# A macaron decoder layer on one core: first rows in turns, norms by Ln and Exp, later a22 splits

## Chip, cores and metric

One core of a Trainium2 chip runs one launch of the kernel. The metric is the device time of that launch in microseconds (us); less is better.

## The reference, cut to what matters

```python
def layer_norm(x, g, b):
    mu = mean(x); var = mean(square(x - mu))
    return (x - mu) * rsqrt(var + 1e-5) * g + b
def swiglu(x, wg, wu, wd):
    return (silu(x @ wg) * (x @ wu)) @ wd
x = layer_norm(ALPHA * x + 0.5 * swiglu(x, ffn1...), ln1)   # D_MODEL 1024, D_FF 2816
proj = x @ w_in                                             # RWKV-7 heads | gated short conv
...
x = layer_norm(ALPHA * x + mix @ w_out, ln2)
x = layer_norm(ALPHA * x + 0.5 * swiglu(x, ffn2...), ln3)   # 512 prompt + 32 sample columns, float32
```

## The kernel before

Activations lie with features on the partitions: z is [128, 8, 544], eight feature tiles by T=544 columns, worked in two halves, HALF = (0, 256) and (256, 544). A float32 product is built from three matmuls in fp32r: weights and inputs are split into a high and a low part, and wh by xh, wh by xl, wl by xh are added in PSUM (mm3, L149 to L151; prod, L464 to L466). The high part is an ACT copy, the low part a DVE subtraction: wsplit (L133, L134) for weights, split (L137, L138) for the rest. So each weight block passes SP's DMA queue, a raw tile, ACT, DVE and then PE.

A feed-forward has 22 tiles of 128 hidden rows in chunks of 4, 4, 4, 4 and 6. The first chunk's up rows are plain products (up, L312 to L338: gate, Silu on ACT, up, a product on DVE), row by row: first() runs the first half's columns, main() the rest. All other work goes in 2x2 blocks with seven products for eight (as Strassen does); each product is 12 matmuls of 272 columns for an "up" item (pairs and its tail, L469 to L545) and 6 for a "down" item (downs, L548 to L581). An item u0 to u5 needs four split weights: b (the block a22), a, y and x. They come from two raw tiles: x and a are loaded by SP (load, L407 and L409), b is split from x (into a tile hlb of its own, L137 and L138), then a DMA on POOL's queue adds the block a11 to x in place (L437), then the y part needs two DVE adds on x (L430, L431). Item results pass through cpb copies on ACT (L525, L531, L534).

What sets the order is a planner: plan() lays the products out in time and gives each part of an item a due time, so many products ahead of its use; feed(), called ahead of each product, issues the loads of the next items as long as fewer than n raw tiles are held, and put() for each part that is due. The engines take their instructions in the order in which they were issued.

```python
LEAD = dict(b=18, a=9, x=7, y=5)
LEAD_B = {0: 25, 1: 23}
```

layer_norm (L191 to L225) takes one half: the column sums by matmuls with ones (L196, L197), the subtraction (L203), squares on ACT (L204), the variance by matmuls (L208, when pair is off), Sqrt on ACT (L218), RECIPROCAL on DVE (L219), a scaling per tile on DVE (L223); the sink then adds the bias and splits into xhl (to_x, L230 on ACT, L231 on DVE) or adds it and stores (to_y, L238). ACT has one function table loaded at a time; L122 and L194 load the next one ahead. Norms are woven with other work (weave): matmuls are issued between their steps; only the last norm, half 0 of ln3 (256 columns), has nothing beside it. rb and xb2 hold multiples of the biases, since z itself is kept without them.

The start (L629 to L646) loads the gate weight of row 0 in four pieces, in turns with x, then the up weight of row 0, both weights of row 1 and the second half of x.

Of the kernel before, what the change touches and what calls it, by code (L numbers as in the profile page):

```python
# [12 lines left out]
F32 = mybir.dt.float32  # L13
# [48 lines left out]
def body(ctx: ExitStack, tc: tile.TileContext, xT, gu1, wd1, win, wo_c, wo_0, wo_1, gu2, wd2, lora, w0, vec, cst,  # L62
# [23 lines left out]
    def col(v, i):  # L86
        return vc[:, v + i:v + i + 1]
# [103 lines left out]
    def layer_norm(z, h, gcol, bcol, epsv, q, rs, s1, sink, pair=True):  # L191
        c0, c1 = HALF[h]
        n = c1 - c0
        ACT.activation(warm, s1[:, 0:1], AF.Sqrt, scale=0.0, bias=one)  # L194
        m = sm()
        PE.matmul(m[:, :n], ones, s1[:, :n], start=True, stop=False)  # L196
        PE.matmul(m[:, :n], ones, z[:, KD - 1, c0:c1], start=False, stop=True)  # L197
        yield 800
        v = sm() if not pair else None
        for j in range(4):  # L200
# [17 lines left out]
        ACT.activation(rs[:, :n], v[:, :n], AF.Sqrt, bias=epsv)  # L218
        DVE.reciprocal(rs[:, :n], rs[:, :n])  # L219
        yield 2600  # L220
        for d in range(KD):
            zz = z[:, d, c0:c1]
            DVE.scalar_tensor_tensor(zz, zz, col(gcol, d), rs[:, :n], op0=OP.mult, op1=OP.mult)  # L223
            sink(d, zz, col(bcol, d), c0, c1)
            yield 800  # L225

    def to_x(z, spill):
        def sink(d, zz, b, c0, c1):
            hi, lo = xhl[:, 0, d, c0:c1], xhl[:, 1, d, c0:c1]
# [1192 lines left out]
```

## Time and profile before

| | us |
|---|---|
| median of 3 runs | 1134.11 (1131.58 to 1135.72) |
| the profiled execution | 1136.22 |
| its span | 1134.5 |

The span is the profiled part of the execution. PE runs matmuls, PEld loads their weights, DVE, ACT and POOL are the other engines, SP only issues DMAs (SPq is its queue). The mean granted clock of PE over the span is 0.995 of full speed. An idle time is put down to the instruction or DMA that ended it ("<-").

### The profile page before, as it was taken

How to read it: one execution, taken by the hardware profiler on the slowest of the kernel's cores; microseconds unless marked ns; L12 is line 12 of the kernel's file. 1: busy time of each engine (PE TensorE's matmuls, PEld its weight loads, DVE VectorE, ACT ScalarE, POOL GpSimd, SP SyncE). 2: the span in 40 equal slices, each digit the busy share in tenths (PEclk: the TensorE clock that was granted, in tenths of full speed). 3: DMA queues.
4: the chain of work that ended last, by engine and by line, in shares of the span. 5: the costliest groups of instructions: out<-in, count | busy, mean ns of one | idle time of the engine just before them, and what ended most of it. 6: DMA issues, size and time to landing. Idle time of an engine off the chain costs nothing.

```text
span 1134.5 us, 22909 instructions
## 1 busy us (share of the span) xinstructions
PE 1099.5 (97%) x9300; PEld 1045.3 (92%) x9300; DVE 851.6 (75%) x1586; ACT 586.2 (52%) x1066; POOL 172.6 (15%) x282
## 2 busy tenths in 40 slices
PE   8999999999999999999999999999999999999995
PEld 7999999999999999898789878899999999999994
DVE  6677888878776857754677467988889887877755
ACT  6545555555553576653345344657455555545513
POOL 0122131302100022230011100001312212130000
PEclk9999999999999999999999999999999999999998
DMA  8558495867753242261228422443866859587302
GB/s 274 129 99 183 110 215 143 170 153 160 175 144 105 81 139 72 52 122 58 68 71 222 119 79 93 169 149 75 166 154 145 192 131 207 130 170 164 98 1 79
DMA packets 97625, 149.31 MB, mean 132 GB/s; under 512 B 35056, under 2 KB 58992, under 8 KB 97520
## 3 DMA queue, kind: packets, MB, share of 16 engines
q1 hardware_dynamic: 70320, 111.67, 32.7%
q0 software_dynamic: 27200, 36.18, 20.4%
q8 instruction: 73, 1.20, 0.4%
q14 instruction: 32, 0.26, 0.1%
HBM read 129.17 MB, written 9.75 MB: 122 GB/s over the span
## 4 chain that ended last, share of the span: by engine, by line
PE 64%; DVE 11%; DMA 10%; issue 9%; ACT 5%; POOL 0%; SPq 0%; ACTq 0%; POOLq 0%; DVEq 0%
PE mm L149 7%; PE mm L464 7%; PE mm L466 6%; PE mm L465 6%; PE mm L151 6%; PE mm L150 6%; DMA raw<-in_gu 5%; PE sm L464 4%; PE sm L466 4%; PE sm L465 4%; DVE hl L134 3%; ACT hl L133 2%; PE sm L929 1%; DMA raw<-in_wd 1%; PE sm L208 1%
## 5 line engine op out<-in xcount | busy, mean ns | idle before, releaser
L134 DVE TENSOR_TENSOR hl<-raw,hl 128x1024 fp32r<-128x1024 f32 (+3 forms) x228 | 269.6, 1189 | 65.6 <-ACT hl L133 64.7
L133 ACT ACTIVATE hl<-raw 128x1024 fp32r<-128x1024 f32 (+3 forms) x228 | 231.5, 1027 | 79.6 <-DVE raw L431 33.3
L149 PE MATMUL mm<-xhl,hl 128*128 128x256 f32 (+1 forms) x768 | 236.2, 308 | 6.8 <-ACT xhl L137 5.0
L151 PE MATMUL mm<-xhl,hl 128*128 128x256 f32 (+1 forms) x768 | 225.6, 295 | 1.4 <-DVE hl L134 1.4
L150 PE MATMUL mm<-xhl,hl 128*128 128x256 f32 (+1 forms) x768 | 224.4, 292 | 0.6 <-DVE xhl L231 0.3
L149 PEld LDWEIGHTS mm<-xhl,hl 128*128 128x128 f32 x768 | 146.0, 190 | 16.1 <-ACT xhl L137 5.3
L151 PEld LDWEIGHTS mm<-xhl,hl 128*128 128x128 f32 x768 | 145.7, 190 | 5.2 <-DVE hl L134 2.2
L150 PEld LDWEIGHTS mm<-xhl,hl 128*128 128x128 f32 x768 | 146.4, 191 | 4.0 <-DVE xhl L138 0.9
L464 PE MATMUL sm<-xhl,hl 128*128 128x272 f32 x432 | 124.8, 289 | 0.0
L466 PE MATMUL sm<-xhl,hl 128*128 128x272 f32 x432 | 124.7, 289 | 0.0
L465 PE MATMUL sm<-xhl,hl 128*128 128x272 f32 x432 | 124.7, 289 | 0.0
L464 PE MATMUL mm<-tv,hl 128*128 128x272 f32 x288 | 84.5, 293 | 4.6 <-ACT cpb L525 3.5
L466 PE MATMUL mm<-tv,hl 128*128 128x272 f32 x288 | 84.2, 292 | 0.0
L465 PE MATMUL mm<-tv,hl 128*128 128x272 f32 x288 | 83.1, 288 | 0.0
L466 PEld LDWEIGHTS sm<-xhl,hl 128*128 128x128 f32 x432 | 81.7, 189 | 0.0
L464 PEld LDWEIGHTS sm<-xhl,hl 128*128 128x128 f32 x432 | 81.5, 189 | 0.0
L465 PEld LDWEIGHTS sm<-xhl,hl 128*128 128x128 f32 x432 | 81.5, 189 | 0.0
L443 POOL DMA_DIRECT2D raw<-in_wd x32 | 39.3, 1495 | 271.4 <-DVE hlb L138 269.6
L437 POOL DMA_DIRECT2D raw<-in_gu x36 | 43.4, 1206 | 239.5 <-DVE hlb L138 132.9
L464 PEld LDWEIGHTS mm<-tv,hl 128*128 128x128 f32 x288 | 54.7, 190 | 6.3 <-ACT cpb L525 4.4
L464 PE MATMUL mm<-hhl,hl 128*128 128x272 f32 x192 | 57.0, 302 | 1.9 <-ACT sv L570 1.8
L464 PE MATMUL sm<-hhl,hl 128*128 128x272 f32 x192 | 55.8, 291 | 0.0
(367 smaller groups left out, 2811.8 us busy)
## 6 DMA issues: line engine op xcount, KB each, us to landing
raw<-in_gu SPq DMA_DIRECT2D x86, 512.0 KB, 5.1
raw<-in_gu POOLq DMA_DIRECT2D x36, 512.0 KB, 7.4
raw<-in_wd SPq DMA_DIRECT2D x32, 512.0 KB, 4.8
raw<-in_win SPq DMA_DIRECT2D x26, 512.0 KB, 3.8
raw<-in_wd POOLq DMA_DIRECT2D x32, 256.0 KB, 6.8
raw<-in_wd SPq DMA_DIRECT2D x16, 384.0 KB, 3.4
z<-cpb POOLq DMA_DIRECT2D x16, 272.0 KB, 9.0
z<-sv POOLq DMA_DIRECT2D x16, 272.0 KB, 5.9
```

Of the source, the lines that this page charges most:

```text
L133: ACT.activation(hl[:, 0, a:b], raw[:, a:b], AF.Copy)
L134: DVE.tensor_tensor(hl[:, 1, a:b], raw[:, a:b], hl[:, 0, a:b].bitcast(F32), op=OP.subtract)
L149: PE.matmul(out, wh, src[:, 0, k, c0:c1], start=(start and i == 0), stop=False)
L150: PE.matmul(out, wh, src[:, 1, k, c0:c1], start=False, stop=False)
L151: PE.matmul(out, wl, src[:, 0, k, c0:c1], start=False, stop=(stop and i == n - 1))
L208: PE.matmul(v[:, :n], ones, qq[:, i, :], start=(j == 0 and i == 0), stop=(j == 3 and i == 1))
L437: POOL.dma_start(x.rearrange("p (s c) -> p s c", s=2), bass.AP(tensor=a11.tensor, offset=a11.offset, ap=[[2 * D, P], [P * 2 * D, 2], [1, 5 ...
L443: POOL.dma_start(four(x)[:, i], bass.AP(tensor=a11.tensor, offset=a11.offset, ap=[[DFF, P], [P * DFF, 2], [1, 256]]), accum_op=OP.add)
L464: PE.matmul(out, wh, src(0, i), start=(first and i == 0), stop=False, skip_group_check=True)
L465: PE.matmul(out, wh, src(1, i), start=False, stop=False, skip_group_check=True)
L466: PE.matmul(out, wl, src(0, i), start=False, stop=(i == n - 1), skip_group_check=True)
L929: PE.matmul(q[r0:r0 + m, o:o + nn], lhs, rhs, start=True, stop=True)
```

## The change

- First rows: rows 0 and 1 of the first feed-forward are computed in turns. The four weights arrive in pieces of two, two and four k tiles, and first_rows runs, for each pair of k tiles, six matmuls for each of four PSUM accumulators. Four matmuls on a zeroed tile and the load of the Silu table stand ahead. The up and gate weights of rows 2 and 3 are loaded ahead of the first down items, and feed() may hold five raw tiles early, not two.
- The a22 split: the lead of part b is 15 products, not 18, for the fourth and later items of a chunk.
- Norms: 1/sqrt is Exp of -0.5 times Ln, both on ACT and in one table. DVE multiplies two tiles at once, ACT applies scale and bias per tile (Identity), and the split takes two tiles. The bias then is in z, and the bias columns rb and xb2 go, so the second feed-forward's inputs are plain splits and the spill holds x with its bias.
- Last norm: three matmuls whose result is not used, two pairs of squares added on DVE (six variance matmuls, not eight), and tiles 3 and 7 scaled on DVE.

```diff
@@ -188,24 +188,32 @@
-    def layer_norm(z, h, gcol, bcol, epsv, q, rs, s1, sink, pair=True):
-        c0, c1 = HALF[h]
+    def layer_norm(z, c0, c1, gcol, bcol, epsv, q, rs, s1, sink, pair=True, table=None, busy=0):
         n = c1 - c0
-        ACT.activation(warm, s1[:, 0:1], AF.Sqrt, scale=0.0, bias=one)
...
+        if busy:
+            o = sm()
+            for _ in range(busy):
+                PE.matmul(o[:, :n], ones, s1[:, :n], start=True, stop=True)
...
-            ACT.activation(qq, zz, AF.Square)
+            sq = ACT.activation(qq, zz, AF.Square)
+            if j == 0 and table == "ahead":
+                tab = issue(sq, ACT.preload_act_table_set, "natural_log_exp_and_others")
             if not pair:
                 yield 900
-                for i in range(2):
-                    PE.matmul(v[:, :n], ones, qq[:, i, :], start=(j == 0 and i == 0), stop=(j == 3 and i == 1))
+                add = busy and j > 1
+                if add:
+                    DVE.tensor_tensor(qq[:, 0, :], qq[:, 0, :], qq[:, 1, :], op=OP.add)
+                nq = 1 if add else 2
+                for i in range(nq):
+                    PE.matmul(v[:, :n], ones, qq[:, i, :], start=(j == 0 and i == 0), stop=(j == 3 and i == nq - 1))
@@ -215,30 +223,34 @@
-        ACT.activation(rs[:, :n], v[:, :n], AF.Sqrt, bias=epsv)
-        DVE.reciprocal(rs[:, :n], rs[:, :n])
-        yield 2600
-        for d in range(KD):
-            zz = z[:, d, c0:c1]
-            DVE.scalar_tensor_tensor(zz, zz, col(gcol, d), rs[:, :n], op0=OP.mult, op1=OP.mult)
-            sink(d, zz, col(bcol, d), c0, c1)
-            yield 800
-
-    def to_x(z, spill):
-        def sink(d, zz, b, c0, c1):
-            hi, lo = xhl[:, 0, d, c0:c1], xhl[:, 1, d, c0:c1]
-            ACT.activation(hi, zz, AF.Identity, bias=b)
-            DVE.scalar_tensor_tensor(lo, zz, b, hi.bitcast(F32), op0=OP.add, op1=OP.subtract)
-            if spill and d % 4 == 3:
-                dma(xsp[:, d - 3:d + 1, c0:c1], z[:, d - 3:d + 1, c0:c1])
+        if table == "late":
+            tab = issue(ACT.activation(warm, v[:, 0:1], AF.Copy), ACT.preload_act_table_set, "natural_log_exp_and_others")
+        ln = ACT.activation(rs[:, :n], v[:, :n], AF.Ln, bias=epsv)
+        if table:
+            after(ln, tab)
+        ACT.activation(rs[:, :n], rs[:, :n], AF.Exp, scale=-0.5)
+        yield 1200
+        for d in range(0, KD, 2):
+            zz = z[:, d:d + 2, c0:c1]
+            DVE.tensor_tensor(zz, zz, rs[:, None, :n].to_broadcast([P, 2, n]), op=OP.mult)
+            for e in (d, d + 1):
+                x, g, b = z[:, e, c0:c1], col(gcol, e), col(bcol, e)
+                if busy and e in (3, 7):
+                    DVE.tensor_scalar(x, x, g, b, op0=OP.mult, op1=OP.add)
+                else:
+                    ACT.activation(x, x, AF.Identity, scale=g, bias=b)
+            sink(d, zz, c0, c1)
+            yield 1600
+
+    def to_x(spill):
+        def sink(d, x, c0, c1):
+            split(xhl[:, 0, d:d + 2, c0:c1], xhl[:, 1, d:d + 2, c0:c1], x)
+            if spill:
+                dma(xsp[:, d:d + 2, c0:c1], x)
         return sink
 
-    def to_y(z):
-        def sink(d, zz, b, c0, c1):
-            ACT.activation(zz, zz, AF.Identity, bias=b)
-            if d % 2:
-                dma(y_o[:, d - 1:d + 1, c0:c1], z[:, d - 1:d + 1, c0:c1])
-        return sink
+    def to_y(d, x, c0, c1):
+        dma(y_o[:, d:d + 2, c0:c1], x)
@@ -248,8 +260,8 @@
-        def __init__(self, z, gu, wd, ph, nf, late=1, rb=None, xb=None):
-            self.z, self.gu, self.wd, self.na, self.nf, self.late, self.rb, self.xb = z, gu, wd, NA, nf, late, rb, xb
+        def __init__(self, z, gu, wd, ph, nf, late=1):
+            self.z, self.gu, self.wd, self.na, self.nf, self.late = z, gu, wd, NA, nf, late
@@ -350,6 +362,21 @@
+        def first_rows(self, o):
+
+            for a, b in ((0, 2), (2, 4), (4, 6), (6, 8)):
+                for i in range(4):
+                    hl = self.w["gu"[i % 2], i // 2]
+                    for k in range(a, b):
+                        for j, (v, y) in enumerate(((0, 0), (0, 1), (1, 0))):
+                            PE.matmul(o[i][:, :256], block(hl, v, k), xhl[:, y, k, 0:256], start=(k == 0 and j == 0),
+                                      stop=(k == KD - 1 and j == 2), skip_group_check=True)
+            for m in range(2):
+                s = self.rows[0][:, m, 0:256]
+                ACT.activation(s, o[2 * m][:, :256], AF.Silu)
+                DVE.tensor_tensor(s, s, o[2 * m + 1][:, :256], op=OP.mult)
+            yield 0
+
@@ -358,28 +385,18 @@
-            def put(hi, lo, x, cols):
-                if cols is None:
-                    split(hi, lo, x)
...
-                put(tv[:, 0, 0, ks], tv[:, 0, 1, ks], ta, b2)
+                split(tv[:, 0, 0, ks], tv[:, 0, 1, ks], ta)
@@ -392,7 +409,7 @@
-                    lead = dict(LEAD, b=LEAD_B.get(key[2], LEAD["b"])) if key[1] == "u" else LEAD
+                    lead = dict(LEAD, b=LEAD_B.get(key[2], LEAD["b"] if key[2] == 2 else 15)) if key[1] == "u" else LEAD
@@ -592,17 +609,17 @@
-                if i == 2 or i == 1 and self.nf == self.na:
+                if i == 1 and self.nf < self.na:
+                    for j, n in enumerate("gu"):
+                        self.w[n, 3] = wload(self.gu[3, :, j, :])
+                elif i in (1, 2):
                     self.t = (-12, -5)[i - 1]
-                    self.feed(2)
+                    self.feed()
...
-                if self.rb is None:
-                    ACT.activation(z[:, d], z[:, d], AF.Copy, scale=2.0 * ALPHA)
-                else:
-                    ACT.activation(z[:, d], z[:, d], AF.Identity, scale=2.0 * ALPHA, bias=self.rb[:, d:d + 1])
+                ACT.activation(z[:, d], z[:, d], AF.Copy, scale=2.0 * ALPHA)
@@ -627,26 +644,43 @@
-    raw, hl = wtiles()
-    f1.w["g", 0] = hl
+    ACT.activation(warm, one, AF.Silu)
+    POOL.memset(cpb[:, 0:256], 0.0)
+    firsts = [sm() for _ in range(4)]
+    for _ in range(4):
+        PE.matmul(firsts[0][:, :256], cpb[:, 0:P], cpb[:, 0:256], start=True, stop=True)
+    ws = [wtiles() for _ in range(4)]
+
+    def first_w(i, a, b):
+        raw, hl = ws[i]
+        dma(raw[:, a * P:b * P], gu1[i // 2, :, i % 2, a * P:b * P])
+        wsplit(hl, raw, a * P, b * P)
+
+    def first_x(a, b, c0, c1):
+        dma(z[:, a:b, c0:c1], xT[:, a:b, c0:c1])
+        split(xhl[:, 0, a:b, c0:c1], xhl[:, 1, a:b, c0:c1], z[:, a:b, c0:c1])
+
+    for a, b in ((0, 2), (2, 4), (4, 8)):
+        first_w(0, a, b)
+        first_x(a, a + 2, 0, 256)
+        first_w(1, a, b)
+        if b - a > 2:
+            first_x(a + 2, b, 0, 256)
+        first_w(2, a, b)
+        first_w(3, a, b)
+    for i, key in enumerate((("g", 0), ("u", 0), ("g", 1), ("u", 1))):
+        f1.w[key] = ws[i][1]
     for k in range(0, KD, 2):
-        dma(raw[:, k * P:(k + 2) * P], gu1[0, :, 0, k * P:(k + 2) * P])
-        dma(z[:, k:k + 2, 0:256], xT[:, k:k + 2, 0:256])
-        wsplit(hl, raw, k * P, (k + 2) * P)
-        split(xhl[:, 0, k:k + 2, 0:256], xhl[:, 1, k:k + 2, 0:256], z[:, k:k + 2, 0:256])
-    f1.w["u", 0] = wload(gu1[0, :, 1, :], 1024, 2)
-    f1.w["g", 1] = wload(gu1[1, :, 0, :])
-    f1.w["u", 1] = wload(gu1[1, :, 1, :])
-    for k in range(0, KD, 2):
-        dma(z[:, k:k + 2, 256:T], xT[:, k:k + 2, 256:T])
-        split(xhl[:, 0, k:k + 2, 256:T], xhl[:, 1, k:k + 2, 256:T], z[:, k:k + 2, 256:T])
+        first_x(k, k + 2, 256, T)
+    for i, n in enumerate("gu"):
+        f1.w[n, 2] = wload(gu1[2, :, i, :])
     dma(vc, vec)
     dma(ones, cst[:, C_ONES:C_ONES + P])
-    drain(f1.first(), f1.main())
+    drain(f1.first_rows(firsts), f1.main())
     lnq = f1.open_lnq()
-    weave("l1a", layer_norm(z, 0, V_LN1G, V_LN1B, epsf, lnq, f1.lnr, f1.s1[0], to_x(z, True)), f1.end())
+    weave("l1a", layer_norm(z, *HALF[0], V_LN1G, V_LN1B, epsf, lnq, f1.lnr, f1.s1[0], to_x(True), table="ahead"), f1.end())
     drain()
-    ln1b = layer_norm(z, 1, V_LN1G, V_LN1B, epsf, lnq, f1.lnr, f1.s1[1], to_x(z, True), False)
+    ln1b = layer_norm(z, *HALF[1], V_LN1G, V_LN1B, epsf, lnq, f1.lnr, f1.s1[1], to_x(True), False)
@@ -654,10 +688,8 @@
-    rb = keep.tile([P, 16], F32, name="rb")
     lo = cpb[:, 0:1024].rearrange("p (a t) -> p a t", a=2)
     sgd = cpb[:, 1024:1600]
-    xb2 = keep.tile([P, KD], F32, name="xb2")
...
-    DVE.tensor_scalar(rb[:, 0:8], vc[:, V_LN1B:V_LN1B + 8], ALPHA, None, op0=OP.mult)
@@ -1089,7 +1117,7 @@
-            if pl:
+            if pl or h:
@@ -1229,7 +1257,7 @@
-    f2 = Ffn(z, gu2, wd2, "2", 4, 0, rb[:, 8:16], xb2)
+    f2 = Ffn(z, gu2, wd2, "2", 4, 0)
...
-                ACT.activation(z[:, k], z[:, k], AF.Identity, scale=ALPHA, bias=rb[:, k:k + 1])
+                ACT.activation(z[:, k], z[:, k], AF.Copy, scale=ALPHA)
@@ -1316,7 +1344,7 @@
-                    (n * FILL["l2a"] for n in layer_norm(z, 0, V_LN2G, V_LN2B, epsl, lnq, lnr, f2.s1[0], to_x(z, False)))))
+                    (n * FILL["l2a"] for n in layer_norm(z, *HALF[0], V_LN2G, V_LN2B, epsl, lnq, lnr, f2.s1[0], to_x(False)))))
@@ -1328,13 +1356,13 @@
-    ln2b = layer_norm(z, 1, V_LN2G, V_LN2B, epsl, lnq, f2.lnr, f2.s1[1], to_x(z, False), False)
+    ln2b = layer_norm(z, *HALF[1], V_LN2G, V_LN2B, epsl, lnq, f2.lnr, f2.s1[1], to_x(False), False, "late")
...
-    weave("l3a", layer_norm(z, 1, V_LN3G, V_LN3B, epsf, lnq, f2.lnr, f2.s1[1], to_y(z)), f2.end())
+    weave("l3a", layer_norm(z, *HALF[1], V_LN3G, V_LN3B, epsf, lnq, f2.lnr, f2.s1[1], to_y, table="ahead"), f2.end())
     drain()
-    drain(layer_norm(z, 0, V_LN3G, V_LN3B, epsf, lnq, f2.lnr, f2.s1[0], to_y(z), False))
+    drain(layer_norm(z, *HALF[0], V_LN3G, V_LN3B, epsf, lnq, f2.lnr, f2.s1[0], to_y, False, busy=3))
     f2.close()
```

SP's queue in the first feed-forward, from the middle of the four down loads on, before. raw_535 and raw_540 are gate and up weight of row 3, raw_681 and raw_683 parts x and a of u0, raw_685 and raw_769 parts x and a of u1, raw_771 part x of u2:

```order
L409 DMA raw_513<-in_wd1 128x2x512
L409 DMA raw_531<-in_wd1 128x2x512
L409 DMA raw_533<-in_wd1 128x2x512
L116 DMA raw_535<-in_gu1 128x1024
L664 DMA sst_4270<-in_sst 128x112
L665 DMA cstate_4271<-in_cstate 128x64
L407 DMA raw_681<-in_gu1 128x1024
L116 DMA raw_540<-in_gu1 128x1024
L407 DMA raw_769<-in_gu1 128x1024
L407 DMA raw_771<-in_gu1 128x1024
L407 DMA raw_683<-in_gu1 128x1024
L407 DMA raw_685<-in_gu1 128x1024
```

After (raw_409 and raw_414 are row 3; raw_547 and raw_565 are u0, raw_567 and raw_787 u1):

```order
L116 DMA raw_409<-in_gu1 128x1024
L116 DMA raw_414<-in_gu1 128x1024
L426 DMA raw_539<-in_wd1 128x2x512
L426 DMA raw_541<-in_wd1 128x2x512
L426 DMA raw_543<-in_wd1 128x2x512
L426 DMA raw_545<-in_wd1 128x2x512
L424 DMA raw_547<-in_gu1 128x1024
L696 DMA sst_4286<-in_sst 128x112
L697 DMA cstate_4287<-in_cstate 128x64
L424 DMA raw_565<-in_gu1 128x1024
L424 DMA raw_567<-in_gu1 128x1024
L424 DMA raw_787<-in_gu1 128x1024
```

Row 3's weights moved ahead of the down loads; u0's a part and u1's x part moved ahead of what comes later.

ACT in the first pairs of the second feed-forward's second chunk, before (raw_9571 is the x part of the fourth item, hlb_9672 its a22 split; cpb copies belong to the items ahead of it):

```order
L525 ACTIVATE cpb_71<-mm_9618 128x272
L531 ACTIVATE cpb_71<-mm_9618 128x272
L137 ACTIVATE hlb_9672<-raw_9571 128x512
L133 ACTIVATE hl_9650<-raw_9360 128x1024
L534 ACTIVATE cpb_71<-mm_9618 128x272
L133 ACTIVATE hl_9705<-raw_9569 128x1024
L525 ACTIVATE cpb_71<-mm_9702 128x272
L489 ACTIVATE hk_8656<-cpb_71 128x272
```

After (raw_9560 and hlb_9706 are the same item's):

```order
L542 ACTIVATE cpb_71<-mm_9607 128x272
L548 ACTIVATE cpb_71<-mm_9607 128x272
L133 ACTIVATE hl_9639<-raw_9265 128x1024
L551 ACTIVATE cpb_71<-mm_9607 128x272
L133 ACTIVATE hl_9690<-raw_9558 128x1024
L542 ACTIVATE cpb_71<-mm_9687 128x272
L137 ACTIVATE hlb_9706<-raw_9560 128x512
L506 ACTIVATE hk_8656<-cpb_71 128x272
```

The a22 split moved from ahead of one item's last copy (L534, now L551) to behind the next item's first copy.

DVE at the tail, from the last addition to z on, before:

```order
L349 TENSOR_TENSOR z_7084<-z_7084,sm_12899 128x256
L223 SCALAR_TENSOR_TENSOR z_7084<-z_7084,vc_66,cpb_71 128x288
L203 TENSOR_TENSOR z_7084<-z_7084,sm_12940 128x2x256 x4
L219 RECIPROCAL cpb_71<-cpb_71 128x256
L223 SCALAR_TENSOR_TENSOR z_7084<-z_7084,vc_66,cpb_71 128x256 x8
```

After:

```order
L361 TENSOR_TENSOR z_7090<-z_7090,sm_12892 128x256
L205 TENSOR_TENSOR z_7090<-z_7090,sm_12924 128x2x256 x4
L213 TENSOR_TENSOR lnq_12720<-lnq_12720 128x256 x2
L235 TENSOR_TENSOR z_7090<-z_7090,cpb_71 128x2x256 x3
L239 TENSOR_SCALAR z_7090<-z_7090,vc_66 128x256
L235 TENSOR_TENSOR z_7090<-z_7090,cpb_71 128x2x256
L239 TENSOR_SCALAR z_7090<-z_7090,vc_66 128x256
```

RECIPROCAL is gone, two additions of squares came in, and eight scalings became four wide products and two tensor_scalar scalings.

## Rows read from the trace of the kernel before

**Rows 1.** page, busy time of each engine
```profile
PE 1099.5 (97%) x9300; PEld 1045.3 (92%) x9300; DVE 851.6 (75%) x1586; ACT 586.2 (52%) x1066; POOL 172.6 (15%) x282
```

**Rows 2.** windows: busy time of each engine by stretch, core 0
```profile
core 0: us, PE busy (x) PEld busy (x) DVE busy (x) ACT busy (x) POOL busy (x), PEclk, DMA share, GB/s
0.00:10.00 10.00, 4.71 (x17) 3.83 (x18) 3.64 (x8) 5.30 (x10) 0.40 (x8) 1.00 0.75 224
10.00:14.00 4.00, 4.00 (x21) 3.91 (x21) 1.89 (x3) 3.74 (x6) 0.00 (x0) 1.00 1.02 363
13.60:21.10 7.50, 7.50 (x65) 7.50 (x65) 6.69 (x10) 4.11 (x7) 0.00 (x0) 1.00 1.06 381
22.00:60.00 38.00, 36.98 (x285) 36.31 (x284) 26.32 (x48) 22.94 (x39) 5.02 (x4) 1.00 0.49 123
60.00:92.00 32.00, 27.72 (x206) 27.07 (x206) 24.99 (x45) 13.06 (x23) 8.47 (x7) 0.95 0.66 134
88.70:91.90 3.20, 3.10 (x13) 3.10 (x14) 3.20 (x6) 0.05 (x1) 1.21 (x1) 0.50 1.12 228
700.00:740.00 40.00, 37.85 (x262) 35.50 (x260) 37.67 (x76) 24.62 (x37) 0.00 (x0) 1.00 0.42 146
...
1119.50:1122.70 3.20, 3.20 (x9) 2.57 (x8) 0.66 (x2) 1.33 (x3) 0.00 (x0) 0.50 0.05 18
```

**Rows 3.** timeline of PE, start: start, duration, line, operation, tiles, count [idle before <-releaser]
```profile
4.80 0.58 PE L149 MATMUL mm<-xhl,hl 128*128 128x256 f32 x1 [4.80 <-ACT xhl L137]
...
12.49 0.41 PE L149 MATMUL mm<-xhl,hl 128*128 128x256 f32 x1
12.70 0.42 PE L150 MATMUL mm<-xhl,hl 128*128 128x256 f32 x1
...
21.14 0.30 PE L149 MATMUL mm<-xhl,hl 128*128 128x288 f32 x1
```

**Rows 4.** waits of PE, 22 to 60 and 60 to 92: us, times, longest
```profile
PE mm L151 <- DVE hl L134: 0.8, 1, 0.8
...
PE mm L464 <- ACT cpb L525: 2.5, 1, 2.5
PE mm L464 <- ACT sv L570: 1.8, 1, 1.8
```

**Rows 5.** timeline of SP's DMA issues, 41 to 73
```profile
43.49 0.33 SPq L116 DMA_DIRECT2D raw<-in_gu  x1
...
69.89 2.64 SPq L407 DMA_DIRECT2D raw<-in_gu  x2
```

**Rows 6.** timeline of ACT, second feed-forward, 818 to 825
```profile
821.55 0.63 ACT L137 ACTIVATE hlb<-raw 128x512 fp32r<-128x512 f32 x1 [3.18 <-DMA raw<-in_gu]
```

**Rows 7.** waits of PE, 815 to 1024
```profile
PE mm L464 <- ACT cpb L534: 3.3, 2, 2.2
```

**Rows 8.** timeline, tail, 1115 to 1137, DVE, PE and ACT
```profile
1117.68 2.48 DVE L203 TENSOR_TENSOR z<-z,sm 128x512 f32<-128x512 f32 x4 [0.36 <-PE sm L197]
...
1119.09 5.41 PE L208 MATMUL sm<-lnq,ones 128*128 128x256 f32 x16 [1.44 <-ACT lnq L204]
...
1124.53 0.47 ACT L218 ACTIVATE cpb<-sm,eps 128x256 f32<-128x256 f32 x1 [3.71 <-PE sm L208]
...
1125.04 1.75 DVE L219 RECIPROCAL cpb<-cpb 128x256 f32<-128x256 f32 x1 [4.88 <-ACT cpb L218]
...
1127.41 3.30 ACT L238 ACTIVATE z<-z,vc 128x256 f32<-128x256 f32 x8 [2.40 <-DVE z L223]
```

**Rows 9.** timelines of POOL and DVE, 158 to 179; landing of L437's DMAs
```profile
159.94 1.21 POOL L437 DMA_DIRECT2D raw<-in_gu  x1 [0.60 <-DVE hlb L138]
...
178.44 0.69 DVE L430 TENSOR_TENSOR raw<-raw 128x512 f32<-128x512 f32 x1
...
DMA to landing us min/median/max: 6.0/7.4/10.1
```

**Rows 10.** groups by line: count, busy us, mean ns, idle before
```profile
L122 ACT ACT_TABLE_LOAD x8 | 10.3, 1283 | 0.1
```

More of the change, by code (lines that the diff above doesn't have):

```diff
@@ L359, in inputs @@
             z11, z12, z21, z22 = (z[:, k:k + HK, t] for k in (0, HK) for t in (lo_t, hi_t))
-            def put(hi, lo, x, cols):
-                if cols is None:
-                    split(hi, lo, x)
-                    return
-                for k in range(2):
-                    ACT.activation(hi[:, k], x[:, k], AF.Identity, bias=cols[:, k:k + 1])
-                    DVE.scalar_tensor_tensor(lo[:, k], x[:, k], cols[:, k:k + 1], hi[:, k].bitcast(F32), op0=OP.add,
-                                             op1=OP.subtract)
             ta, *nt1 = (cpb[:, a * TB:(a + 2) * TB].rearrange("p (k t) -> p k t", k=2) for a in (0, 2, 4))
@@ L372, in inputs @@
                 ks = slice(k, k + 2)
-                b2, db = (None, None) if self.xb is None else (self.xb[:, ks], self.xb[:, HK + k:HK + k + 2])
                 n1 = nt1[k // 2]
@@ L376, in inputs @@
                 DVE.scalar_tensor_tensor(ta, n1, -1.0, z22[:, ks], op0=OP.mult, op1=OP.subtract)
-                put(tv[:, 0, 0, ks], tv[:, 0, 1, ks], ta, b2)
+                split(tv[:, 0, 0, ks], tv[:, 0, 1, ks], ta)
                 DVE.scalar_tensor_tensor(ta, ta, -1.0, z21[:, ks], op0=OP.mult, op1=OP.subtract)
-                put(tv[:, 2, 0, ks], tv[:, 2, 1, ks], ta, None)
+                split(tv[:, 2, 0, ks], tv[:, 2, 1, ks], ta)
                 yield 0
                 DVE.tensor_tensor(ta, z22[:, ks], z12[:, ks], op=OP.subtract)
-                put(tv[:, 1, 0, ks], tv[:, 1, 1, ks], ta, db)
+                split(tv[:, 1, 0, ks], tv[:, 1, 1, ks], ta)
                 yield 0
@@ L668, in body @@
     DVE.tensor_scalar(der, vc[:, V_KA:V_KA + 4], -1.0, 1.0, op0=OP.mult, op1=OP.add)
-    DVE.tensor_scalar(rb[:, 0:8], vc[:, V_LN1B:V_LN1B + 8], ALPHA, None, op0=OP.mult)
-    DVE.tensor_scalar(xb2[:, 0:HK], vc[:, V_LN2B + HK:V_LN2B + KD], -1.0, None, op0=OP.mult)
-    DVE.tensor_tensor(xb2[:, HK:KD], vc[:, V_LN2B + HK:V_LN2B + KD], vc[:, V_LN2B:V_LN2B + HK], op=OP.subtract)
-    DVE.tensor_scalar(rb[:, 8:16], vc[:, V_LN2B:V_LN2B + 8], 2.0 * ALPHA, None, op0=OP.mult)
     T12, kf, rf, vf = (pp.tile([P, 576], F32, name=n) for n in ("T12", "k", "r", "v"))
```

## Prediction

> **What bounds the kernel now.** The page's first part comes first: PE is busy for 1099.5 us of the 1134.5 us span [rows 1], so in most of the run only fewer matmuls could help, and the change removes next to none. What is to be had is the 35 us in which PE stands still, and the stretches at a granted clock of 0.50. Next I read the windows for where these lie [rows 2]: some at the start, 1.0 in 22 to 60, 4.3 in 60 to 92, 2.2 in 700 to 740. In each I asked the waits, or the timeline of the releasing engine, what ended the idle time [rows 4, 6, 7], and for a load when it was issued [rows 5]. Last came the tail, where nothing is left to overlap and each engine's row starts where another's ends [rows 8]. The profiled execution took 1136.2 us, 2.1 above the median of the runs (1134.1); I sum against the first and move the result by 2.1.
>
> **Start.** The first matmul starts at 4.80; rows 0 and 1 over the first 256 columns are 96 matmuls, done when the first 128x288 matmul begins at 21.14 [rows 3]. Early matmuls follow each other at 0.21 (12.49 to 12.70), later ones at 7.50/65 = 0.115 [rows 2, 3]; 256 columns at 1.2 and at 2.4 GHz, though the clock column gives 1.00 for both stretches; here the pace tells the level. Afterwards all four weights and the half of x (4 x 512 + 4 x 256 KiB = 3.15 MB) must land before the last quarter can run. At 224 GB/s throughout that is 14.0 us; at 2.24 MB by 10 us and 363 GB/s after it, 12.5 [rows 2]. I take 13.3. The last weight's split is an ACT piece of 0.63 and a DVE piece of 0.69 (128x512) [rows 6, 9]: 14.6. Behind it stand the last six matmuls of the third batch, 0.7, and the 24 of the fourth, 2.8, at 0.115: 18.1. **Gain 3.0** (2.3 to 3.8). The four warm matmuls and the Silu table load lie before any weight lands and cost nothing; without that cover the matmuls, 4 x 2 x 0.427 at the pace of the last norm's [rows 8], would cost up to 3.4 and the table 1.28 [rows 10].
>
> **First loads behind it.** The weight of m=3 was issued at 43.49, behind four down loads; PE lost 0.8 to its DVE split and 0.2 more in 22 to 60 [rows 2, 4, 5]. It now goes ahead of them, as the SP rows above show. **Gain 1.0.** In 60 to 92 PE stood 4.3, in two waits of 1.8 and 2.5 [rows 2, 4]. The releasers named are ACT results, but the cause is the order on SP's queue: u0's a part and u1's x part were issued last, from 69.89 on [rows 5], behind two raws of later items. Now the order is natural and all five raws may be asked for earlier. The pause also took the clock to 0.50 in 88.7 to 91.9, where 13 matmuls took 3.2 [rows 2]; at 0.115 to 0.125 they take 1.6, so 1.6 goes too. Of 5.9 I allow 0.5 for a new short wait: **gain 5.4** (0 to 5.9). The four down loads each move two places back; their products stand behind all up rows of the first chunk, so I cost that at nothing; uncovered it would be part of the 0.5.
>
> **Later a22 split.** The a22 split moves three products back in 12 places (the fourth item of three chunks, items four to six of the last, in both feed-forwards). In the second feed-forward ACT met it twice before its raw tile had landed: the first time ACT idled 3.18 ahead of 821.55 [rows 6]. The copy L534 stood behind it, and PE lost 3.3 to that copy in two waits [rows 7]. Now the split stands behind that copy, as the ACT rows show, and the raw tile has 36 matmuls more to land, 36 x 36.98/285 = 4.7 us [rows 2], which covers the 3.18. **Gain 3.2** (0 to 3.3). What follows the split moves as well: the accumulating DMA on POOL's queue comes up to 4.7 later. At the tightest place it was issued at 159.94, the slowest landing takes 10.1, and the add that needs it began at 178.44 [rows 9]: 8.4 of slack, 3.7 left. I cost that at nothing; without that cover it is rival 4.
>
> **Norms.** Per half, eight DVE scalings and eight DVE low parts (0.4 each) become four wide products and four wide low parts (0.69 each), and RECIPROCAL (1.75) an ACT Exp [rows 8, 9]: DVE loses 6.4 + 1.75 - 5.5 = 2.6 us, and ACT gains four wide splits at 0.63, 2.5, and an Exp [rows 6, 8]. Where others fill PE this is worth nothing. It shows in 700 to 740, where DVE is busy 37.67 of 40 and PE stands 2.15 [rows 2]: I take half, since the work also leaves ACT later. **Gain 1.1** (-1 to 2.2). The added table load between variance and Ln in the second half of LN2 is covered by the first rows' matmuls; if not, it costs 1.28 [rows 10]. The second feed-forward's inputs lose eight bias steps on each engine for four wide ones, beside the same matmuls: nothing.
>
> **Tail.** The last norm's variance ran from 1119.09 to 1124.50, part of it at 0.50 (1119.5 to 1122.7), 16 PE records for eight matmuls, 0.427 a record there [rows 2, 8]; PE had stood 1.44 before. Now three dummies fill that pause and DVE adds two pairs of squares, so six matmuls remain: at 2.4 GHz 6 x 2 x 0.213 = 2.6, ending with the last square and its add at about 1121.6. That is 2.9. With the clock down as before, six take 5.1 and the gain is 0.3. I take the first, for the pause is what stands ahead of the fall. Sqrt and RECIPROCAL, 1124.53 to 1126.8, become Ln and Exp at 0.47 each and a hand-over: 1.3 less. Scaling, bias and store ran to 1130.71, 3.9; now DVE's chain is four products at 0.69 and two scalings at about 0.41, 3.6: 0.3 less. **Gain 4.5** (1.9 to 5.0).
>
> **Sum:** 3.0 + 1.0 + 5.4 + 3.2 + 1.1 + 4.5 = 18.2. I hold back 0.7 for stalls that come back where PE now arrives sooner: 17.5, so 1118.7 against the profiled time and **1116.6** against the median.
>
> **Rivals.**
> 1. *The loads' wait moves on.* The raw ring still has five tiles and DMA the same bytes; if the tiles of the first chunk are late in the new order too, the 5.4 is lost: gain 12.1, **1122**. For it: DMA is at 134 GB/s in 60 to 92 [rows 2], far from the 363 it reached, so the queue was held by tiles, not bytes. Against it: u0 and u1 now come first.
> 2. *Taking turns starves PE at the start.* Each batch of 24 matmuls takes 24 x 0.115 = 2.8 warm, but its weights and x, 0.79 MB, take 3.5 at 224 GB/s. If PE's pauses hold the clock at 1.2 GHz, a batch takes 24 x 0.21 = 5.1, and four from 4.8 end at 25.0: 3.9 lost instead of 3.0 won, **1123.5**; with half of the batches slow, some 1121. For it: the clock fell behind the pause at 86 and behind the 1.44 at 1119. Against: it rose by 13.6 in the old start, with PE busy 4.71 of the first 10 us [rows 2]. The Trainium skill (TensorE: Matmul & The Clock Gate, "HAM oscillation — how this bites in real kernels") speaks for this rival: a loop whose work per k tile is shorter than the wait for the next tile drops the clock at every tile, and all k tiles of one row should run before the next wait, the opposite of taking turns. By that rule the time would be the 1123.5; the old start shows one rise and no fall.
> 3. *ACT becomes the bound of the norms.* In the four halves that feed matmuls ACT gets 2.5 for splits and 0.5 for Exp more each [rows 6, 8]. If all 12.0 were exposed, 5.5 of gain would be left, **1128.6**, no change. Against it: ACT is busy 24.62 of 40 in 700 to 740 [rows 2].
> 4. *The later split makes the y part late.* If the accumulating DMA lands too late by more than the 3.7 left, PE waits in each of 12 places, by up to 4.7 us: 56. Beyond 17.5 + 5.7 = 23 lost, 1.9 a place, the kernel is slower; at the full 56 it takes **1173**. Against it: the landing of 10.1 is the longest seen [rows 9].
>
> **How the numbers follow.** Forecast 0.62, rival 1 0.17, rival 2 0.10, rival 3 0.07, rival 4 0.04. A measurement of this kernel can tell about 0.5%, 5.7 us, from no change, so faster means under 1128.4: the first three cases, 0.89; the same is rival 3, 0.07; slower rival 4, 0.04. The forecast's low end adds the upper bounds of start, LN2, tail and the feed-forward waits, 0.8 + 1.1 + 0.5 + 0.1, the 1.2 held back, and 2.1 for the spread of runs, 5.8 in all: 1110.8. Its high end loses LN2's and the tail's lower bounds, 2.1 + 2.6: 1121.3. Rivals 1 and 2 reach to 1122 to 1124, and with the cold tail to 1127: range, rounded outward, 1110 to 1127.
>
> **What would show it.** Right: the first 128x288 matmul near 18.1, with matmuls 0.115 apart from about 10 us; waits on L525's and L570's successors (L542, L587) gone in 60 to 92, and no 0.50 there; ACT idle before the a22 split, if any, behind the cp copy near 824; variance matmuls at 0.21 a record; some 9 us from the last sum to the last store's issue, instead of 13. Wrong: matmuls 0.21 apart up to the end of the first rows, new waits on tiles between 45 and 110, PE waiting for the y parts' splits, or ACT as releaser of xhl after the norms.

## The result and the profile after

| | before | after |
|---|---|---|
| median | 1133.78 us (4 runs, 1131.58 to 1135.72) | 1116.76 us (4 runs, 1115.19 to 1122.3) |
| ratio | | 0.9845, 95% interval 0.9812 to 0.9877 |
| profiled execution: span | 1134.5 us | 1113.4 us |

The medians lie 17.0 us apart, the spans of the two profiled executions 21.1: that of after was the fastest of its four runs. From the page of after, the row that answers to [rows 1]:

```profile
PE 1093.4 (98%) x9310; PEld 1040.5 (93%) x9310; DVE 836.0 (75%) x1540; ACT 590.1 (53%) x1077; POOL 172.9 (16%) x283
```

PE is busy 6.1 us less with ten more records: part of that is time at 1.2 GHz that is gone. Its idle time fell from 35.0 to 20.0. The windows of after, for the stretches that answer to [rows 2] (columns as there):

```profile
0.00:10.00 10.00, 8.55 (x41) 6.76 (x42) 4.23 (x10) 5.59 (x12) 0.65 (x9) 1.00 0.70 211
10.00:14.00 4.00, 3.66 (x29) 3.31 (x28) 2.85 (x6) 3.23 (x6) 0.00 (x0) 1.00 1.05 374
...
22.00:57.00 35.00, 35.00 (x279) 35.00 (x278) 26.74 (x48) 22.36 (x40) 5.02 (x4) 1.00 0.57 135
57.00:88.00 31.00, 31.00 (x246) 30.60 (x245) 27.37 (x47) 16.05 (x28) 8.50 (x7) 1.00 0.84 173
685.00:725.00 40.00, 39.58 (x293) 37.76 (x292) 36.26 (x73) 24.68 (x41) 0.00 (x0) 1.00 0.44 147
```

PE is busy 35.00 of 35 and 31.00 of 31 where it stood 1.0 and 4.3 before, the clock stays at 1.00 there, and around the second norm it stands 0.4 instead of 2.2. PE's timeline at the start, then the tail on PE, ACT and DVE, answer to [rows 3] and [rows 8]:

```profile
1.25 3.70 PE L651 MATMUL sm<-cpb 128*128 128x256 f32 x8 [1.25 <-POOL cpb L648]
5.08 7.18 PE L372 MATMUL sm<-xhl,hl 128*128 128x256 f32 x49
12.60 5.77 PE L372 MATMUL sm<-xhl,hl 128*128 128x256 f32 x47 [0.34 <-DVE xhl L138]
18.21 0.29 PE L149 MATMUL mm<-xhl,hl 128*128 128x288 f32 x1
```

```profile
1100.37 1.03 PE L199 MATMUL sm<-cpb,ones 128*128 128x256 f32 x4
1101.98 2.95 PE L216 MATMUL sm<-lnq,ones 128*128 128x256 f32 x12 [0.58 <-ACT lnq L206]
...
1104.97 0.47 ACT L228 ACTIVATE cpb<-sm,eps 128x256 f32<-128x256 f32 x1 [1.25 <-PE sm L216]
1105.47 0.42 ACT L231 ACTIVATE cpb<-cpb 128x256 f32<-128x256 f32 x1
...
1105.92 1.90 DVE L235 TENSOR_TENSOR z<-z,cpb 128x512 f32<-128x512 f32 x3 [1.75 <-ACT cpb L231]
1107.73 0.41 DVE L239 TENSOR_SCALAR z<-z,vc 128x256 f32<-128x256 f32 x1
1108.06 0.69 DVE L235 TENSOR_TENSOR z<-z,cpb 128x512 f32<-128x512 f32 x1
1108.78 0.41 DVE L239 TENSOR_SCALAR z<-z,vc 128x256 f32<-128x256 f32 x1
```

The first 128x288 matmul is at 18.21 (18.1 was forecast). In the tail 4.36 pass from the first subtraction (1100.57) to the end of the variance, where before it was 6.8; from the start of Ln (before: Sqrt) to DVE's first product 0.95 pass, where it was 2.3.

To see where the time went, both programs are cut at the same matmuls. LN1, LN2 and LN3 are the three norms; "sums" are the matmuls with ones that begin one half of a norm, and LN2 runs here from the sums of its first half to those of its second. Two kernels were run again, so there are two traces of before and three of after:

| stretch, us | before | after | predicted gain | gain of means |
|---|---|---|---|---|
| start to first 128x288 | 21.14, 20.97 | 18.21, 18.39, 18.18 | 3.0 | 2.8 |
| to first down product | 38.68, 38.43 | 36.60, 36.60, 36.60 | 1.0 | 2.0 |
| to end of second chunk's downs | 92.04, 93.35 | 86.02, 86.01, 86.02 | 5.4 | 6.7 |
| to sums of LN1, second half | 234.06, 234.43 | 234.49, 232.65, 234.70 | 0 | 0.3 |
| projections and mixing, to LN2 | 319.29, 321.48 | 317.85, 323.45, 319.24 | 0 | 0.2 |
| LN2 | 33.56, 33.63 | 31.58, 31.57, 31.58 | 1.1 | 2.0 |
| second feed-forward, to the last sums | 377.26, 376.91 | 374.33, 374.04, 373.71 | 3.2 | 3.1 |
| tail | 18.43, 16.74 | 14.35, 14.35, 14.37 | 4.5 | 3.2 |
| span | 1134.5, 1135.9 | 1113.4, 1117.1, 1114.4 | 17.5 | 20.2 |

Some stretches repeat within 0.1 us; the mixing differs by 5.6 between traces of one kernel. So the experiments are read by stretches and waits. Those called e2, e3 and e5 to e8 have one execution each (1117.20, 1117.13, 1125.72, 1121.86, 1125.25 and 1121.71 us), and e6 and e8, whose other stretches are near those of the changed kernel, lie 5 above its median by a mixing of 325: such single times settle nothing.

### The profile page after: what moved, and what is told of

The parts are those of the page before. It is cut to its first block, busy times and chain, and to the rows that moved or that the text cites. A ratio compares the mean times of both kernels' runs of the same rounds, so it can differ in the third digit from the quotient of the medians.

```text
span 1113.4 us, 22923 instructions
## 1 busy us (share of the span) xinstructions
PE 1093.4 (98%) x9310; PEld 1040.5 (93%) x9310; DVE 836.0 (75%) x1540; ACT 590.1 (53%) x1077; POOL 172.9 (16%) x283
## 4 chain that ended last, share of the span: by engine, by line
PE 79%; issue 7%; DMA 4%; DVE 4%; ACT 4%; POOL 1%; SPq 0%; ACTq 0%; POOLq 0%; DVEq 0%
PE mm L149 10%; PE mm L151 9%; PE mm L150 9%; PE mm L481 7%; PE mm L482 7%; PE mm L483 7%; PE sm L483 5%; PE sm L482 5%; PE sm L481 5%; DMA raw<-in_gu 2%; ACT hl L133 1%; PE sm L957 1%; DVE hl L134 1%; PE sm L150 1%; PE sm L149 1%
## 5 line engine op out<-in xcount | busy, mean ns | idle before, releaser
L134 DVE TENSOR_TENSOR hl<-raw,hl 128x1024 fp32r<-128x1024 f32 (+3 forms) x232 | 270.4, 1171 | 72.6 <-ACT hl L133 71.8
L149 PE MATMUL mm<-xhl,hl 128*128 128x288 f32 (+1 forms) x736 | 224.3, 305 | 0.3 <-DVE z L1324 0.3
L150 PE MATMUL mm<-xhl,hl 128*128 128x288 f32 (+1 forms) x736 | 214.1, 291 | 0.0
L151 PE MATMUL mm<-xhl,hl 128*128 128x288 f32 (+1 forms) x736 | 213.9, 292 | 0.2 <-DVE hl L134 0.2
L149 PEld LDWEIGHTS mm<-xhl,hl 128*128 128x128 f32 x736 | 138.3, 188 | 8.3 <-issue 2.6
L151 PEld LDWEIGHTS mm<-xhl,hl 128*128 128x128 f32 x736 | 138.0, 188 | 4.0 <-issue 1.6
L150 PEld LDWEIGHTS mm<-xhl,hl 128*128 128x128 f32 x736 | 138.4, 188 | 2.8 <-DVE xhl L138 0.4
```

What stands on the lines that cost most here:

```text
L134: DVE.tensor_tensor(hl[:, 1, a:b], raw[:, a:b], hl[:, 0, a:b].bitcast(F32), op=OP.subtract)
L149: PE.matmul(out, wh, src[:, 0, k, c0:c1], start=(start and i == 0), stop=False)
L150: PE.matmul(out, wh, src[:, 1, k, c0:c1], start=False, stop=False)
L151: PE.matmul(out, wl, src[:, 0, k, c0:c1], start=False, stop=(stop and i == n - 1))
```

## The experiments

**The start, in three kernels.** The first undoes both parts (start of before), the second adds the four matmuls to it, the third keeps the turns and drops the four matmuls.

```diff
-    drain(f1.first_rows(firsts), f1.main())
+    drain(f1.first(), f1.main())        # e1, e2: loads in the order of before
...
-    for _ in range(4):                  # e1, e3
-        PE.matmul(firsts[0][:, :256], cpb[:, 0:P], cpb[:, 0:256], start=True, stop=True)
```

> The changed kernel with the start of before: gate weight of row 0 first, rows one after the other, no matmuls ahead (the Silu table load stays first). Theory (the start is worth 2.9 by itself and the rest of the gain does not hang on it): the first 128x288 matmul at 21.1 as before, not 18.2, matmuls 0.21 apart until about 13, and the time 2.9 above the changed kernel, some 1119.7. Rival (the sooner start only moves PE into later waits for loads): the first 128x288 matmul at 21.1, but the 3 us are made up by the first down product (54.8 in the changed kernel), and the time is within 1 us of 1116.8.

> As the last one, with the four matmuls on a zeroed tile ahead, but rows 0 and 1 one after the other. Theory of the prediction (the bytes bound the start; the last weight lands at 13 to 14, a whole-tile split of 1.05 and 1.2 follows and 24 matmuls at 0.117, 2.8): the first 128x288 matmul at about 18.5 to 19, so the warm-up is worth 2.3 or more of the 2.9 and the turns under 0.6. Rival (the turns matter, since rows one after the other need whole weights): about 20.5 to 21, and the warm-up alone is worth under 0.6.

> The changed kernel without the four matmuls on a zeroed tile; rows 0 and 1 still in turns. Theory (turns leave pauses, and without warm-up the clock rises only after some 8 us of work, as in before): matmuls 0.21 apart until about 13, the first 128x288 matmul at 20 to 21. Rival 2 of the prediction (turns keep the clock down throughout): 0.21 up to the end of the first rows, the first 128x288 matmul at about 25. Other rival (bytes bound it anyway): still 18.2 to 18.8.

The first 128x288 matmul came at 20.53, 20.92 and 19.01 (18.21 with both). So the turns are worth 1.5 without the warm-up and 2.7 with it; the warm-up is worth 0.8 with turns, and without them nothing. These are single traces, and in the nine whose start is that of the changed kernel this matmul comes between 17.66 and 18.73: the turns' 2.7 is clear of that, the warm-up's 0.8 is not. The forecast for e3 missed: not 20 to 21, and matmuls 0.21 apart only until 9 (35 of them ran in 9 to 13), not 13. The lines are from PE's timeline and the windows of e2:

```profile
6.42 0.27 PE L151 MATMUL mm<-xhl,hl 128*128 128x256 f32 x1
7.59 0.39 PE L149 MATMUL mm<-xhl,hl 128*128 128x256 f32 x1 [0.90 <-ACT xhl L137]
8.32 0.39 PE L150 MATMUL mm<-xhl,hl 128*128 128x256 f32 x1 [0.34 <-DVE xhl L138]
...
5.00:9.00 4.00, 2.62 (x13) 1.92 (x13) 2.19 (x5) 1.88 (x5) 0.00 (x0) 1.00 0.94 307
9.00:13.00 4.00, 3.95 (x20) 3.50 (x19) 2.61 (x5) 2.69 (x5) 0.00 (x0) 0.59 1.01 359
```

Row 0 alone has six matmuls per piece of x, PE stands 0.90 and 0.34 for the next one, and the clock that the warm-up had raised is down again (0.59 in 9 to 13). The theory for e2, that the bytes bound the start and the turns are worth under 0.6, falls. In e1, the 128x288 matmuls and all later work up to the second chunk simply came 2.3 later (first down product at 57.13), so the loss is not made up by then and the rival falls; 2.9 was expected. Its median was 1118.85, 0.8 to 2.7 above the three medians of the changed kernel, though the spread of the runs is as large.

**The changed kernel again**, twice (the second beside e9 and e10).

> The changed kernel once more, as a yardstick for what differs between two traces of one kernel. Expected: the first 128x288 matmul at 18.2, first down product at 54.8, last norm's sums at 1099, each within 0.5; time 1115 to 1118. If the waits at 287 (1.4), 866 (1.5) and 1053 (1.2) come from the time that an accumulating DMA or a load happens to take, they differ here by more than 0.5; if from the order of the queues, they are the same within 0.2.

> The changed kernel beside the last two on the same chip, as their yardstick: 1116 to 1119; clock 0.66 in the 10 us behind the 1.17 wait near 568.

Medians 1118.08 and 1116.16. The wait at 287 was 1.4, absent and 1.1 in the three traces, that at 1053 1.2, 0.45 and absent; the one at 866 was 1.5, 1.5 and 1.4, but 0.2 in e1 and absent in e2 and e3, whose second feed-forward is written alike. So all three seem to hang on how long a DMA happens to take, not on the order of the queues alone; the third varies less than the others. The clock after the 1.17 wait near 568 was 1.00, 0.66 and 1.00: the 0.66 expected for e11 did not come. Windows of e4, behind its waits of 1.39 and 1.17:

```profile
450.00:460.00 10.00, 9.52 (x71) 8.44 (x72) 4.40 (x9) 3.56 (x10) 0.77 (x5) 0.66 0.42 93
569.50:579.50 10.00, 9.87 (x67) 8.20 (x68) 4.45 (x10) 3.04 (x8) 0.08 (x1) 0.66 0.35 95
```

At 0.66 over 10 us, 6.8 us ran at 0.50, which costs at most half of it, 3.4. The first trace of after has neither fall, and its mixing is 5.6 shorter: 2.8 for each, if all of the difference is theirs.

**The loads of the first feed-forward, in two kernels.** e5 undoes both edits of main(), e6 only the early raw tiles.

```diff
-                if i == 1 and self.nf < self.na:                        # e5
-                    for j, n in enumerate("gu"):
-                        self.w[n, 3] = wload(self.gu[3, :, j, :])
-                elif i in (1, 2):
+                if i == 2 or i == 1 and self.nf == self.na:
                     self.t = (-12, -5)[i - 1]
-                    self.feed()                                         # e5, e6
+                    self.feed(2)
```

> The changed kernel with the load order of before inside the first feed-forward: row 3's weights behind the down loads, feed(2) ahead of the first items. Theory (that order made the waits in 22 to 60 and in 60 to 92): from the first 128x288 matmul to the first down product 38.6 instead of 36.6, from there to the end of the second chunk's downs 92 instead of 86.0, with waits of some 2 near the first up items and a granted clock of 0.50 behind the longer; in all 6 to 8 us more by then. Rival 1 (the sooner start or the tile ring decides, not the order): both stretches as in the changed kernel within 1 us.

> The changed kernel with feed(2) instead of feed() ahead of the first items in both feed-forwards; row 3's weights stay ahead of the down loads. Theory (two parts: row 3's place is worth 2.1, the five early raw tiles the rest): 36.6 up to the first down product as in the changed kernel, but 90 to 92 from there to the end of the second chunk's downs instead of 86.0. Rival (row 3's place alone brought u0 and u1 forward, five tiles add nothing): 36.6 and 86.0. In the second feed-forward no difference over 0.5 by either.

e5: 38.8 and 91.2, times 1125.72 (span 1124.0). e6: 36.6 and 86.0, as in the changed kernel. PE's waits in 19 to 160, of e5 and then of e6:

```profile
PE mm L481 <- ACT sv L587: 2.2, 1, 2.2
PE mm L481 <- ACT cpb L542: 1.2, 1, 1.2
PE mm L149 <- ACT hl L133: 0.9, 1, 0.9
PE mm L151 <- DVE hl L134: 0.8, 1, 0.8
```

```profile
PE mm L481 <- ACT cpb L542: 0.2, 1, 0.2
```

e5 and e6 differ in nothing but the place of row 3's weights, so that place is worth 7.4 by itself; the rival of e6 holds, five raw tiles add nothing here. In e5 SP issues its loads in the pattern of before, in e6 in that of after although the tiles are two. What put u1 and u2 ahead of u0's a part would then be row 3's up weight, which was issued between the item loads and took a place in the ring; this last step is read from the order of the loads, not tried apart.

**The a22 split 18 products ahead.**

```diff
-LEAD["b"] if key[2] == 2 else 15
+LEAD["b"]
```

> The changed kernel with the a22 split of the fourth and later items 18 products ahead again. Theory (ACT stands before that split until its load lands, and the cp copy L551 behind it holds PE): waits of PE on L551 return in the second feed-forward, 2 to 4 us in all near 808 and 1002, and perhaps 0.7 near 282; from the second norm's last sums to the third norm's first sums 355 to 357 instead of 351 to 354. Rival (the waits went because loads come at other times now): no wait on L551 over 0.5, and 351 to 354.

```profile
PE mm L481 <- ACT cpb L551: 5.7, 4, 2.5
```

That row is from PE's waits in 19 to 1100: 1.5 at 86, 0.7 at 283, 1.0 at 817 and 2.5 at 1012. From the second norm's last sums to the third norm's first it took 357.04, against 353.6 to 354.2 in the three traces of after. The wait on L551 occurs nowhere in those, so the theory holds, and the part is worth more than its term. The 1.5 at 86 was not forecast: the stretch from the first down product to the end of the second chunk's downs takes 87.8 here instead of 86.0, so part of the gain there belongs to the later split.

**No unused matmuls in the last norm.**

```diff
-            for _ in range(busy):
-                PE.matmul(o[:, :n], ones, s1[:, :n], start=True, stop=True)
```

> The changed kernel without the three matmuls in the last norm whose result is not used; two pairs of squares are still added on DVE. Theory of the prediction (the pause ahead of the squares lets the clock fall): variance matmuls 0.43 apart, granted clock 0.50 for some 3 us in the tail, and 16.5 to 17 from the last norm's sums to the end instead of 14.1 to 14.4. Rival (six matmuls instead of eight and the shorter chain did it): 0.21 apart, 14.0 to 14.4.

```profile
1108.48 2.95 PE L212 MATMUL sm<-lnq,ones 128*128 128x256 f32 x12 [1.44 <-ACT lnq L202]
```

That row is from e8's timeline of PE. The pause of 1.44 is back, the twelve records still take 2.95, and sums to end took 14.29. The rival holds here. The second trace of before says why [rows 8] read otherwise:

> The kernel before, a second trace of it. Theory (its waits at 76.7, 86.0, 823 and 1019 come from the queues' order): each there again within 0.5 us; granted clock 1.00 behind its 0.56 wait near 579. Open: whether the clock falls to 0.50 in the tail behind the 1.44 pause again; if it does, the matmuls that fill this pause are worth some 2 us on average, if not, less.

```profile
1122.26 3.72 PE L208 MATMUL sm<-lnq,ones 128*128 128x256 f32 x16 [1.44 <-ACT lnq L204]
```

The row is from PE's timeline of e12: behind the same pause the clock did not fall, and the 16 records took 3.72 where they had taken 5.41. Of four traces with this pause (before, e8, e10, e12) one shows the fall; the 1.7 it costs is what the three matmuls may save now and then. The waits on L570 and L525 came again at 76 and 85 (1.6, 2.7), those on L534 at 827 and 1023 (1.2, 1.7); the clock behind 579 was 1.00.

**Waits that remain, in two kernels.** PE waits 1.17 at 568 for the score products' PSUM buffers: on DVE a weight split (L134) now stands ahead of the products L868, as DVE's timeline of after shows:

```profile
566.73 1.22 DVE L134 TENSOR_TENSOR hl<-raw,hl 128x1024 fp32r<-128x1024 f32 x1
567.87 0.45 DVE L1134 TENSOR_TENSOR O<-gq,sm 128x288 f32<-128x288 f32 x1
568.23 2.88 DVE L868 TENSOR_TENSOR SC<-sm,cs 128x512 f32<-128x512 f32 x6
```

In before that split came behind them (582.21, after products from 579.05 on). The condition `pl or h`, by which the second group norm lost its table load, is the likely cause of the new order. e9 puts the load back, and frees two buffers:

```diff
-            if pl or h:
+            if pl:
...
-            cps = [cpb[:, 0:T], cpb[:, T:2 * T], self.rows[1][:, 0], self.rows[1][:, 1]]
+            blocks = cpb[:, 0:6 * TB].rearrange("p (a t) -> p a t", t=TB)
+            rt = lambda c: c.rearrange("p (r t) -> p r t", r=2)
+            cps = [blocks[:, 0:2], blocks[:, 2:6:3], rt(self.rows[1][:, 0]), rt(self.rows[1][:, 1])]
...
-                s = self.rows[0] if ci < LAST and j == 0 else sv
+                s = self.rows[j % 2]
```

> The changed kernel with three edits: the table load ahead of the Ln in the second group norm is back (as in before), so that DVE's order near 566 is that of before; the down items' cpb results lie in blocks 0, 1, 2 and 5 of cpb, so that the next item's first two copies need not wait for the accumulating DMA; the last chunk's first item uses the rows of hk, not those of sv. Theory (a 1.17 wait of PE for a DVE product that stands behind a split and the group norm lets the clock fall; the copies wait for a DMA that still reads their tile): near 568 a wait of about 0.55, granted clock 1.00 in the 10 us behind it (0.66 in eight of nine traces with the 1.17 wait); waits on L542 under 0.2 everywhere, none on L548 near 287; 4 to 6 us less than the changed kernel, some 1112 to 1113. Rival (the clock falls there whatever the wait, and the copies wait for something else): clock 0.66 behind 568 again, waits on the copies as before, time within 1 us of the changed kernel.

Median 1112.29 (1109.59 to 1114.71, 5 runs), ratio to before 0.9792 (0.9771 to 0.9813), where e11 beside it has 0.9831 (0.9811 to 0.9851). PE's timeline and the window behind it:

```profile
569.58 0.85 PE L867 MATMUL sm<-AR,bkb 64*128 64x128 f32 x4 [0.56 <-DVE SC L870]
...
568.00:578.00 10.00, 9.44 (x101) 8.28 (x99) 8.30 (x17) 3.05 (x8) 0.71 (x4) 1.00 0.39 110
```

The wait is 0.56 with the clock at 1.00, and on DVE the split stands behind the products again. The waits at 287 and 866 do not occur, but neither do they in some traces without the new buffers, so one trace does not show that these removed them; those on L542 at 208 (0.6) and 273 (0.2) stay, where under 0.2 was expected, and so does one of 0.8 on L548 near 1053. Its median lies 3.9 below e11's (4 to 6 was expected), the lowest of all kernels here; the intervals overlap by a little.

e10 lets other matmuls in between the score groups and also drops the unused matmuls of the last norm:

```diff
-                yield 0
+                yield 600
```

> As the last one, and the score products yield 600 ns to other matmuls between their groups (not 0), and the last norm has no unused matmuls. Theory: the 1.39 wait near 450 and the 0.55 near 568 and 588 go, with the fall of the clock behind the first (0.66 over 10 us in five of nine traces); 1.5 to 4 less than the run above, some 1109 to 1111; the tail as long as with the unused matmuls, 14.1 to 14.4, if the clock falls there only now and then, or 2 more if it falls. Rival (the fill taken there is missing later, where the background work runs out): the waits go, and others of the same length come before 700; time within 1 us of the run above.

```profile
PE sm L955 <- DMA DM<-Dd: 3.9, 2, 2.7
PE mm L149 <- ACT hl L133: 1.5, 1, 1.5
```

From PE's waits in 22 to 1100. The waits on the score products are gone, but other waits come: 2.7 at 494, 1.2 at 623, 1.5 near 720, and LN2 takes 37.3 instead of 31.8 in e9. So the rival holds for the waits, but not for the time. The median is 1124.41 (1116.9 to 1130.34), 12 above e9 and not within 1. The trace is of one of the shortest runs (1117.47), and the mean clocks of the seven go from 0.998 down to 0.985; what lengthens the others no trace shows.

## Why the prediction was right, step by step

The median was forecast at 1116.6 and is 1116.76. The terms agree less well than the sum.

- *Start, 3.0:* 2.8, right in size and time (18.1, 18.2). The bound by bytes was only half of the reason: ACT begins the last weight's split at 13.94 in after and at 13.89 in e2 (13.3 was forecast for the landing), and yet without the turns the first rows end at 20.5 to 20.9. Rival 2 had it the wrong way round: four times the matmuls per piece of x keep PE fed. The row-by-row order of e1 and e2, the nearest here to running all k tiles of a row before the next wait, loses 2.3 to 2.7. That was the advice of the Trainium skill (TensorE: Matmul & The Clock Gate, "HAM oscillation — how this bites in real kernels"); the trace of e2 agrees with that section that waits between k tiles can drop the clock (0.59 in 9 to 13), but it does so in the row-by-row order, where x arrives in pieces too.
- *Row 3's weights, 1.0:* 2.0, mis-sized. I summed PE's idle time in 22 to 60. The stretch took 38.68 for matmuls that need 36.60, and only 1.0 of the difference is booked as idle: around each wait some matmuls start late within the modelled end of the one before, and seven late starts come to 1.9.
- *First chunk's end, 5.4:* 6.7 (6.0 between the profiled executions), and the cause was given wrongly in part. "All five raw tiles may be asked for earlier" is worth nothing (e6). Where row 3's weights stand gives 5.2 of it, and the 2.0 ahead of it (e5 against e6); undoing the later a22 split alone costs 1.8 in the same stretch (e7), about the rest, and the sum had put nothing there for it. Rival 1 did not occur: PE is busy 31.00 of 31 in 57 to 88.
- *Later split, 3.2, and 0.7 held back:* 3.1 in the stretch. Undone, it brings 5.7 of waits back, 2.2 of them in the first feed-forward (e7). In the trace of after new waits of 1.5 and 1.2 stand near 866 and 1053, more than the 0.7; that the split caused them is not shown. Rival 4 did not occur: no wait on a y part.
- *Norms, 1.1:* 2.0, near the upper bound. Taking half for fear of ACT was too careful: ACT is busy 24.68 of 40, as before, and PE stands 0.4 there in all. Rival 3 falls with it. No run undoes this part alone, so its 2.0 rests on the comparison of stretches, which repeat within 0.1.
- *Tail, 4.5:* 4.1 between the profiled executions, 2.4 against the second trace of before. The 2.9 for the variance measured 2.45, and even that only because this one profile of before had the clock down. The unused matmuls added nothing that e8 or e10 shows. Ln and Exp gave 1.35 (1.3), the wide products 0.1 (0.3).
- *Not in the sum:* the condition `pl or h`, which I passed over, went with a DVE split ahead of the score products and a wait of PE near 568 of 1.17 instead of 0.56. Behind it the clock fell in eight of ten traces. By estimate that is 0.6 + 0.8 x 2.8 = 2.8 lost on average which no term had; in those ten traces the mixing took 322.2 on average, before it took 319.3 and 321.5. This loss helped the sum to fit although three terms were too small, so that the median came out within 0.2 is in part luck.
- *Stretches and medians:* the stretches give 20, the medians of the three comparisons 16 to 19. The profiled executions of before (1136.2 and 1137.7) lie above its median, and two of the three of after had no fall near 568.

That e9's 3.9 comes from the table load rather than the buffers was not tried apart; 2.8 for the first and 1.4 for the wait at 866 are read from traces, not from separate runs.

## What to carry to other kernels

Cut two traces at the same matmuls and compare stretches: idle time undercounts what late weights cost, and a sum that fits can hide terms that don't. Where a load stands among others in a queue with a ring of tiles can matter more than how many tiles there are. When something late feeds several rows, work on all of them per piece; a warm-up ahead gained nothing in e2, where PE then waited.

## What was not expected of the hardware

The same pause is followed by a fall of the clock in some runs of the same kernel and not in others: 8 of 10 traces behind the 1.17 wait near 568, 7 of 13 behind the 1.39 wait near 450, none of three behind the 0.56 wait, one of four behind the 1.44 pause of the tail. Near 568 each fall lasted 6.8 us (0.66 over 10) and cost some 2.8; near 450 most did, one half as long. So most of the spread of one kernel's runs (1115.19 to 1122.3, with mean clocks of 0.997 and 0.989) may be a count of such falls, and a single trace says little of what a pause costs. That taking pauses away narrows the spread is not shown: five runs of e9 lie within 5.1, five of e11 within 3.3, seven of e10 within 13.4.
